# A hybrid decoder step on one core: stages placed by a clock of every engine's queue, and the sample recurrence in small tiles

## The chip, the cores and the metric

The kernel runs on one core of one Trainium2 chip. A core has TensorE (PE, matrix products into PSUM), VectorE (DVE), ScalarE (ACT), GpSimd (POOL) and SyncE (SP, which here issues the transfers). The metric is the device time of one execution in microseconds; the time given is the median of several runs. The profile shown is of one execution.

## The reference, cut to what matters

One layer is applied to a prompt of 1024 tokens and to a sample group of 8 sequences with 8 new tokens each, 1088 tokens in all. The order is: a SwiGLU feed-forward half step, a token mixer, a second SwiGLU half step, each followed by a layer norm.

```python
x = _layer_norm(ALPHA * x + 0.5 * _swiglu(x, ffn1_w13, ffn1_w2), ln1_g, ln1_b)
y, S, nk, nv = _mixer(x, S0, buf_k, buf_v, lb, w_in, attn_sink, attn_norm_g, hgrn_norm_g, w_out)
x = _layer_norm(ALPHA * x + y, ln2_g, ln2_b)
x = _layer_norm(ALPHA * x + 0.5 * _swiglu(x, ffn2_w13, ffn2_w2), ln3_g, ln3_b)
```

The mixer projects x to 22 groups of 128 columns. 8 attention heads with 2 key/value heads look at a window of 128 tokens. Four recurrent heads (HGRN2) keep a state S of 128 x 128 for each sequence:

```python
f = lb + (1.0 - lb) * sigmoid(hf);  logf = log(f);  k = 1.0 - f
# per chunk: b = cumsum(logf)
o = einsum('bthk,bhkv->bthv', qc * exp(b), S)
a = einsum('bthk,bshk,btshk->bhts', qc, kc, exp(b_t - b_s where s <= t))
o = o + einsum('bhts,bshv->bthv', a, vc)
S = exp(b_last)[..., None] * S + einsum('bshk,bshv->bhkv', kc * exp(b_last - b), vc)
```

Prompt states start at zero, sample states at the given S0. Both groups' outputs are normalised, gated, joined and multiplied by w_out.

## The kernel before, in words

**Layout and large products.** Tokens stand in three chunks of columns, 512, 288 and 288 (`CH`); the 64 sample tokens are columns 1024 to 1087. A large product splits both operands into a high and a low part and takes three products of these with `mmr` (line 207): high by high, high by low, low by high. `hilo` makes the two parts of a weight tile, a copy on ACT (L408) and a subtraction on DVE (L409). The feed-forward products use the Strassen-like seven-product scheme in most places (`seven`) and plain products elsewhere. Small products of the mixer are full float32 matmuls through `mm` (line 203), each of which the hardware shows as two matmul instructions, and transposes go through `tr` (line 211).

**The order of work.** All instructions are emitted by one Python program that keeps an estimated PE time `s.t`: every `mm`, `mmr` and `tr` adds its assumed length. The main stream is a list of units (`run`); in the mixer a unit is one 128-column projection, which `proj_group` computes chunk by chunk. Everything beside it is a `Side`, a Python generator: layer norms, attention blocks, the four recurrent heads, the splits of the mixer's results. A side runs until its next `yield x`, which says that its next stage is due `x` nanoseconds later on `s.t`. The main stream calls `poll` at each of its own yields, twice for each chunk of a projection (`mm3` yields after half the pieces, 12 matmuls); `poll` emits at most three due stages. PE works through its instructions in the order emitted, so a stage emitted before its operands are there makes PE wait, with the projections behind it. `need`, `until` and `room` emit stages at once when the main stream cannot go on.

**PSUM and rows.** Stages take PSUM banks from a pool of five (`st`), projections from one of three (`pt`). SBUF is used as 32 rows of 128 x 1152 floats; attention's tiles share the pool of weight tiles `hl`.

**Attention.** `attn_block` handles 128 prompt queries in stages: scores, exponentials, transposes and products with v, norm, transpose back. One block starts the next. `attn_sample` handles the sample tokens in four groups. The delays are numbers such as 400, 2100, 4500, 1200.

**The recurrent heads.** `hgrn(h)` starts when head h's F, Q and V projections are there. Within 128 tokens the decayed products are built by halving: first the diagonal (`hgrn_a`), then seven levels with blocks of 1, 2, 4 up to 64 tokens (`LEV`). At each level PE multiplies KL by QR for the blocks (`hgrn_b`; for the sample tokens at the first three levels `hgrn_c`, a product of 64 x 32 in its own bank). Then DVE multiplies half of QR by the decays (L1557), POOL half of KL (L1558), DVE forms the decays of the next level (L1564) and puts the level's products where they belong (L1573, L1583). The next level reads the new KL and QR. A level ends in `yield 1800.0`. Then KL is transposed, the chunk states are formed (`hgrn_d`) and the outputs (`hgrn_e`). For the sample tokens, eight products of a state with 8 columns of QR give a transposed result (`hgrn_f`), a copy to SBUF follows, and `hgrn_g` adds the part within the sequence and the transpose back. The new sample states are Ks times Ve, two products of 512 columns (`hgrn_i`); Ve holds the values of each sequence, masked by `em`, side by side.

**After the heads.** `wout_a` multiplies the attention half of the mix by w_out while head 3 is still running; `oa_split` and `oh_split` prepare these operands on ACT (L441) and DVE (L442). `wout_b` adds the recurrent half and starts the second layer norm.

## Time and profile before

| what | value |
|---|---|
| median of 3 runs | 2102.89 us (2102.34 to 2106.88) |
| the profiled execution | 2100.44 us, its span 2098.7 us |
| TensorE clock granted | 0.996 of full speed |
| PE busy | 2050.0 us, 98% of the span |
| DVE, ACT, POOL busy | 1214.9, 834.5, 178.3 us |

A busy row of PE counts overlapping matmuls once. A row such as `1024.00 2.94 PE pp L207 x12` of a timeline or of the chain gives the start, the length and the number of merged instructions; `[0.43 <-DVE Q L1557]` behind a row is idle time of its engine before it and what ended it. [...] A row of the waits gives the engine and line that waited, what released it, and total, times and longest in us.

### The profile page before, as it was taken

How to read it: one execution, taken by the hardware profiler on the slowest of the kernel's cores; microseconds unless marked ns; L12 is line 12 of the kernel's file. 1: busy time of each engine (PE TensorE's matmuls, PEld its weight loads, DVE VectorE, ACT ScalarE, POOL GpSimd, SP SyncE). 2: the span in 40 equal slices, each digit the busy share in tenths (PEclk: the TensorE clock that was granted, in tenths of full speed). 3: DMA queues.
4: the chain of work that ended last, by engine and by line, in shares of the span. 5: the costliest groups of instructions: out<-in, count | busy, mean ns of one | idle time of the engine just before them, and what ended most of it. 6: DMA issues, size and time to landing. Idle time of an engine off the chain costs nothing.

```text
span 2098.7 us, 40231 instructions
## 1 busy us (share of the span) xinstructions
PE 2050.0 (98%) x16089; PEld 1933.8 (92%) x16089; DVE 1214.9 (58%) x2463; ACT 834.5 (40%) x1886; POOL 178.3 (8%) x353
## 2 busy tenths in 40 slices
PE   8999999999999999999999999999999999999998
PEld 8999999998899999878888888998999999888997
DVE  7766555555357552465644767576666655444855
ACT  5443333334336443444443233454343333432521
POOL 0000000000020210022213201300000000000121
PEclk9999999999999999999999999999999999999999
DMA  6332222227357331101111132342222222655832
GB/s 236 96 103 88 88 75 80 70 81 236 118 165 237 90 111 62 31 22 39 36 53 38 47 124 64 105 139 83 88 83 95 91 78 74 209 159 165 272 104 93
DMA packets 126124, 221.97 MB, mean 106 GB/s; under 512 B 14336, under 2 KB 44032, under 8 KB 125920
## 3 DMA queue, kind: packets, MB, share of 16 engines
q1 hardware_dynamic: 125936, 219.39, 33.0%
q8 instruction: 126, 2.06, 0.4%
q14 instruction: 62, 0.51, 0.1%
HBM read 181.69 MB, written 38.63 MB: 105 GB/s over the span
## 4 chain that ended last, share of the span: by engine, by line
PE 40%; DVE 6%; ACT 2%; issue 2%; DMA 1%; POOL 1%; DVEq 0%; SPq 0%; ACTq 0%; POOLq 0%
PE py L207 13%; PE u L207 7%; PE y L207 5%; PE pp L207 5%; PE pg L207 2%; PE pu L207 2%; DVE hl L409 2%; PE z L207 1%; ACT hl L408 1%; PE nat L211 1%; PE hgrn_b L203 1%; PE hgrn_e L203 0%; PE attn_block_c L203 0%; DMA raw<-in_w2tb 0%; ACT ev L918 0%
## 5 line engine op out<-in xcount | busy, mean ns | idle before, releaser
L207 PE MATMUL py<-g,hl 128*128 128x288 f32 (+3 forms) x3234 | 540.9, 327 | 6.8 <-DVE hl L409 4.6
L207 PEld LDWEIGHTS py<-g,hl 128*128 128x128 f32 x3234 | 487.4, 188 | 55.0 <-DVE hl L409 9.5
L409 DVE TENSOR_TENSOR hl<-raw,hl 128x512 fp32r<-128x512 f32 (+1 forms) x600 | 387.8, 659 | 224.4 <-ACT hl L408 222.5
L408 ACT CAST hl<-raw 128x512 fp32r<-128x512 f32 (+1 forms) x600 | 351.7, 593 | 404.9 <-PE py L207 187.0
L207 PE MATMUL u<-T,hl 128*128 128x288 f32 (+1 forms) x2700 | 365.3, 291 | 6.0 <-ACT ev L1049 5.0
L207 PEld LDWEIGHTS u<-T,hl 128*128 128x128 f32 x2700 | 349.9, 189 | 10.0 <-ACT ev L1049 7.9
L207 PE MATMUL pp<-Xh,hl 128*128 128x288 f32 (+1 forms) x1056 | 272.2, 335 | 0.0
L207 PEld LDWEIGHTS pp<-Xh,hl 128*128 128x128 f32 x1056 | 182.7, 189 | 19.9 <-issue 5.0
L207 PE MATMUL pp<-Xl,hl 128*128 128x288 f32 (+1 forms) x528 | 173.1, 328 | 0.0
L634 POOL TENSOR_SCALAR lnt<-lnr,lnp 128x1 f32<-128x1 f32 (+1 forms) x81 | 41.2, 508 | 1510.8 <-DVE lnr L630 843.0
L918 ACT ACTIVATE ev<-ev 128x288 f32<-128x288 f32 (+1 forms) x150 | 65.0, 434 | 258.3 <-DVE ev L1054 171.4
L207 PE MATMUL z<-B,hl 128*128 128x288 f32 (+1 forms) x900 | 121.8, 290 | 2.1 <-DVE ev L1054 2.1
L207 PE MATMUL y<-T,hl 128*128 128x288 f32 (+1 forms) x900 | 122.0, 290 | 0.6 <-DVE T L467 0.6
L207 PE MATMUL u<-B,hl 128*128 128x288 f32 (+1 forms) x900 | 121.7, 290 | 0.0
L207 PE MATMUL y<-B,hl 128*128 128x288 f32 (+1 forms) x900 | 121.7, 290 | 0.0
L207 PEld LDWEIGHTS z<-B,hl 128*128 128x128 f32 x900 | 117.0, 189 | 2.3 <-DVE ev L1054 2.3
L207 PEld LDWEIGHTS y<-T,hl 128*128 128x128 f32 x900 | 117.1, 189 | 0.8 <-DVE T L467 0.8
L207 PEld LDWEIGHTS y<-B,hl 128*128 128x128 f32 x900 | 117.0, 189 | 0.0
L207 PEld LDWEIGHTS u<-B,hl 128*128 128x128 f32 x900 | 117.0, 189 | 0.0
L207 PEld LDWEIGHTS pp<-Xl,hl 128*128 128x128 f32 x528 | 99.8, 189 | 6.2
L409 DVE TENSOR_TENSOR hl<-S,hl 128x512 fp32r<-128x512 f32 x88 | 60.9, 692 | 74.8 <-ACT hl L408 74.4
L207 PE MATMUL py<-oH,hl 128*128 128x288 f32 (+1 forms) x384 | 96.5, 332 | 1.4 <-DVE Y L1836 1.4
(273 smaller groups left out, 2404.8 us busy)
## 6 DMA issues: line engine op xcount, KB each, us to landing
raw<-in_w13b SPq DMA_DIRECT2D x120, 256.0 KB, 3.2
raw<-in_w13a SPq DMA_DIRECT2D x108, 256.0 KB, 3.2
raw<-in_w2ta SPq DMA_DIRECT2D x75, 256.0 KB, 3.6
raw<-in_w2tb SPq DMA_DIRECT2D x75, 256.0 KB, 3.5
gd<-go SPq DMA_DIRECT2D x44, 288.0 KB, 3.2
raw<-gd SPq DMA_DIRECT2D x88, 144.0 KB, 3.3
gd<-go SPq DMA_DIRECT2D x44, 256.0 KB, 3.5
raw<-gd SPq DMA_DIRECT2D x44, 256.0 KB, 4.5
```

The source lines that it names most:

```text
L203: s.nc.tensor.matmul(out, lhsT, rhs, start=start, stop=stop, skip_group_check=cols > 1)
L207: s.nc.tensor.matmul(out, lhsT, rhs, start=start, stop=stop, skip_group_check=loose)
L211: s.nc.tensor.transpose(out, in_, ident)
L408: lambda: nc.scalar.copy(hl[:, 0, :nb], src),
L409: lambda: nc.vector.tensor_tensor(hl[:, 1, :nb], src, hl[:, 0, :nb].bitcast(F32), ALU.subtract),
L634: e.tensor_scalar(t, r, r, hp, ALU.mult, ALU.mult)
L918: nc.scalar.activation(si, ps, AF.Silu)
```

## The change

**Clock.** `Ker` gets a `Clock`, and its engines are wrapped (`Watch`) so that every instruction emitted is also booked. DVE, ACT, POOL and SP each have a time from which they are free. An operation is booked to start when its engine is free and 50 ns after the last booked write of its operands, and to take a length given by `COST`. Transfers are booked on SP and on one bus. `pe`, which `mm`, `mmr` and `tr` now call, moves `s.t` on to the booked arrival of the operands before it adds the matmul's length. `fresh` tells the clock when a pool's tile is reused.

**Stages.** Most yields in attention and in the recurrent heads no longer give a delay but the tiles that the next stage's matmuls read, and in many cases the number of PSUM banks that it takes. Such a stage is due 100 ns after these tiles are booked as written and when the banks are booked as free (`due`). Layer norms, the splits and the feed-forward parts keep their numbers.

**Assumed lengths.** Small matmuls on a quarter or half of the array (`cols`) are now counted at a quarter or half of their length in the scores of the sample attention and in the recurrence; before, these were counted in full. An `mmr` is counted 0.5 ns longer.

**Sample recurrence.** `hgrn_c` goes: the sample tokens are handled in two blocks of 32 tokens in the bank and the tile shape of `hgrn_b`, also in `hgrn_a`, and pass through a ninth column of D. `hgrn_f` and the copy behind it go: QR of the sample tokens is copied into `qm`, a zeroed tile in which each sequence's 8 columns have 32 of their own, and `hgrn_g` accumulates the state products directly, in two halves of 32 rows of its result. `hgrn_i` becomes two pairs of products of 32 rows of Ks with 256 columns of Ve, which is now half as wide.

The diff, cut to its core (the other yields of attention, `need`, `until`, `room` and `need_hl` change in the same way; other tile allocations get the `fresh` shown for attention's):

```diff
+class Clock:
...
+    def there(s, ap):
+        lo, hi = s.span(ap)
+        return max((t for a, b, t in s.wrote.get(ap.name, ()) if a < hi and b > lo), default=0.0)
...
+    def write(s, ap, t):
+        lo, hi = s.span(ap)
+        s.wrote[ap.name] = [x for x in s.wrote.get(ap.name, ()) if x[0] < lo or x[1] > hi] + [(lo, hi, t)]
+        s.use(ap, t)
...
+    def fresh(s, ap, tag, bufs):
+        q = s.tags.setdefault(tag, [])
+        q.append(ap.name)
+        if len(q) > bufs:
+            t = s.used.get(q.pop(0), 0.0)
+            s.wrote[ap.name] = [(0, 1 << 30, t)]
+            s.held[ap.name] = t
+        return ap
+    def soonest(s, tag, bufs, n=1):
+        q = s.tags.get(tag, [])
+        i = len(q) + n - 1 - bufs
+        return s.used.get(q[i], 0.0) if 0 <= i < len(q) else 0.0
...
+    def run(s, e, cost, outs, ins):
+        t = max([s.free[e]] + [s.there(x) + s.HOP for x in ins + outs]) + cost
+        s.free[e] = t
+        for x in ins:
+            s.use(x, t)
+        for x in outs:
+            s.write(x, t)
+        for x in ins + outs:
+            s.held[x.name] = t
...
+    def dma(s, out, in_):
+        t = max(s.free["SP"], s.there(in_) + s.HOP, s.there(out) + s.HOP) + 450.0
+        s.free["SP"] = t
+        n = 1
+        for a, b in out.ap:
+            n *= b
+        s.bus = max(s.bus, t + 800.0) + n * 4 / 330.0
+        s.use(in_, s.bus)
+        s.write(out, s.bus + 600.0)
...
+COST = dict(
+    DVE=lambda op, n: 160.0 + 0.62 * n if op in ("tensor_scalar", "tensor_copy", "memset") else 150.0 + 1.05 * n,
+    ACT=lambda op, n: 195.0 + 0.78 * n,
+    POOL=lambda op, n: 100.0 + 0.85 * n if op == "memset" else 340.0 if n == 1 else 190.0 + 2.7 * n,
+)
...
+        def g(*a, **k):
+            r = f(*a, **k)
+            if op == "dma_start":
+                s.clock.dma(a[0], a[1])
+                return r
+            aps = [x for x in [*a, *k.values()] if hasattr(x, "free_size")]
+            outs = [aps.pop(0)]
+            cost = COST[s.name](op, max(x.free_size() for x in [*outs, *aps]))
+            if "accum_out" in k:
+                outs.append(k["accum_out"])
+                cost += 190.0
+            s.clock.run(s.name, cost, outs, aps)
+            return r
...
+    def pe(s, out, lhsT, rhs, cost):
+        c = s.clock
+        t = max(s.t, c.there(lhsT) + c.HOP, c.there(rhs) + c.HOP, c.held.get(out.name, 0.0) + c.HOP)
+        s.wait(out, lhsT, rhs, t)
+        s.t = t + cost
+        c.use(lhsT, s.t)
+        c.use(rhs, s.t)
+        c.write(out, s.t + 200.0)
...
     def mm(s, out, lhsT, rhs, start, stop, cols=1):
         n = out.free_size()
-        s.t += 2 * (max(111.0, n * (2 / 2.4) + 24.0) if cols == 1 else (n * (2 / 2.4) + 24.0) / cols)
+        s.pe(out, lhsT, rhs, 2 * (max(111.0, n * (2 / 2.4) + 24.0) if cols == 1 else (n * (2 / 2.4) + 24.0) / cols))
         s.nc.tensor.matmul(out, lhsT, rhs, start=start, stop=stop, skip_group_check=cols > 1)
...
     def mmr(s, out, lhsT, rhs, start, stop, loose=False):
-        s.t += out.free_size() / 2.4 + 12.5
+        s.pe(out, lhsT, rhs, out.free_size() / 2.4 + 13.0)
...
         else:
-            d.ready = s.t + (lat or 0.0)
+            if lat is None or isinstance(lat, float):
+                d.ready = s.t + (lat or 0.0)
+            else:
+                d.banks = 0
+                d.ready = 0.0
+                for x in lat if isinstance(lat, tuple) else (lat,):
+                    if isinstance(x, int):
+                        d.banks = x
+                    else:
+                        d.ready = max(d.ready, s.clock.there(x) + 100.0)
+                return
+            d.banks = 0
...
+    def due(s, d):
+        return max(d.ready, s.clock.soonest("ps", 5, d.banks) if d.banks else 0.0)
...
         for d in list(s.sides):
-            if most and d.ready <= s.t:
+            if most and s.due(d) <= s.t:
...
             assert s.hl_live + s.as_live <= NHL, "scores"
-            pr = s.wh.tile([P, 2, 512], F32, tag="hl", name=s.nm("as"))
+            pr = s.clock.fresh(s.wh.tile([P, 2, 512], F32, tag="hl", name=s.nm("as")), "hl", NHL)
...
             if jp == 0:
-                yield 400.0
+                yield (2,)
...
-        yield 2100.0
+        yield nm
...
-        yield 4500.0
+        yield sx[0, 0][:, : 256 + w], 2
...
-            if q < 4:
-                yield 1200.0
+            if q < 3:
+                yield pb, sx[order[q + 1]][:, : 256 + w], 1
+            elif q == 3:
+                yield pb
...
-        yield 1000.0
...
+        yield KL, QR, 1
+        nc.gpsimd.memset(A, 0.0)
...
-                s.mm(ps[32 * b : 32 * b + 32, c * 32 : c * 32 + 32], KL[:, sl], QR[:, sl], True, True)
-        nc.vector.tensor_tensor(D, ps[:, :256].rearrange("p (c t) -> p c t", c=8), s.i32.unsqueeze(1).to_broadcast([P, 8, 32]), ALU.mult)
-        ps = s.st("hgrn_a_")
-        sl = slice(1024, 1088)
-        s.mm(ps[:64, :64], KL[:, sl], QR[:, sl], True, True)
-        nc.vector.tensor_tensor(A[:64, sl], ps[:64, :64], s.ident[:64, :64], ALU.mult)
+                s.mm(ps[32 * b : 32 * b + 32, c * 32 : c * 32 + 32], KL[:, sl], QR[:, sl], True, True, cols=4)
+        for b in range(2):
+            sl = slice(1024 + 32 * b, 1056 + 32 * b)
+            s.mm(ps[32 * b : 32 * b + 32, 256:288], KL[:, sl], QR[:, sl], True, True, cols=4)
+        nc.vector.tensor_tensor(D[:, :8], ps[:, :256].rearrange("p (c t) -> p c t", c=8), s.i32.unsqueeze(1).to_broadcast([P, 8, 32]), ALU.mult)
+        nc.vector.tensor_tensor(D[:64, 8], ps[:64, 256:288], s.i32[:64], ALU.mult)
         nc.vector.tensor_tensor(QR, QR, F, ALU.mult)
-        yield 4000.0
+        yield KL, QR, 1
...
-                        s.mm(ps[k0 : k0 + m, c * m : (c + 1) * m], KL[:, c0 : c0 + m], QR[:, c0 + m : c0 + 2 * m], True, True)
+                        s.mm(ps[k0 : k0 + m, c * m : (c + 1) * m], KL[:, c0 : c0 + m], QR[:, c0 + m : c0 + 2 * m], True, True, cols=64 // m)
...
-                    s.mm(ps[32 * b : 32 * b + 32, c * 16 : c * 16 + 16].rearrange("p (x m) -> p x m", m=m), KL[:, k0 : k0 + 32], v(QR[:, k0 : k0 + 32], 32, 1), True, True)
+                    s.mm(ps[32 * b : 32 * b + 32, c * 16 : c * 16 + 16].rearrange("p (x m) -> p x m", m=m), KL[:, k0 : k0 + 32], v(QR[:, k0 : k0 + 32], 32, 1), True, True, cols=4)
             if smp:
-                p2 = s.st("hgrn_c_")
-                s.mm(p2[:64, :32].rearrange("p (x m) -> p x m", m=m), KL[:, 1024:1088], v(QR[:, 1024:1088], 64, 1), True, True)
+                for b in range(2):
+                    k0 = 1024 + 32 * b
+                    s.mm(ps[32 * b : 32 * b + 32, 128:144].rearrange("p (x m) -> p x m", m=m), KL[:, k0 : k0 + 32], v(QR[:, k0 : k0 + 32], 32, 1), True, True, cols=4)
...
-                yield 1800.0
+                yield KL, QR, 1
...
+            for q, r in ((P, slice(0, 8)), (64, slice(8, 9)))[: 2 if smp else 1]:
+                k = r.stop - r.start
+                nc.vector.copy_predicated(
+                    D[:q, r].rearrange("p c (x u m) -> p c x u m", u=2, m=m)[:, :, :, 1],
+                    s.l32[:q, li].rearrange("p (x m) -> p x m", m=m).unsqueeze(1).to_broadcast([q, k, 16 // m, m]),
+                    ps[:q, r.start * 16 : r.stop * 16].rearrange("p (c x m) -> p c x m", c=k, m=m),
+                )
...
+                    nc.scalar.copy(A[bs, :1024].rearrange("p (c t) -> p c t", c=8)[:, :, bs], D[bs, :8])
+                    if b < 2:
+                        nc.scalar.copy(A[bs, 1024 + 32 * b : 1056 + 32 * b], D[bs, 8])
...
-            yield 1800.0
+            yield KL, QR, 1
...
-        yield 1300.0
+        yield F, Vn, 1
...
-            yield 1500.0
+            if g == 0:
+                yield 400.0
+            else:
+                yield A, S[:, :384], 1
...
-            yield 200.0
-        ps = s.st("hgrn_f_")
-        for b in range(8):
-            s.mm(ps[:, b * 8 : (b + 1) * 8], S0[:, b * P : (b + 1) * P], QR[:, 1024 + 8 * b : 1032 + 8 * b], True, True)
-        it = s.t2("it")
-        nc.scalar.copy(it[:, :64], ps[:, :64])
-        yield 500.0
+            if g == 0:
+                yield S, 1
+        nc.vector.tensor_copy(s.qm.rearrange("p g (b x) -> p g b x", b=4)[:, :, :, :8], QR[:, 1024:1088].rearrange("p (g b t) -> p g b t", g=2, b=4))
+        yield s.qm, S0, 1
         ps = s.st("hgrn_g_")
-        s.mm(ps[:64, :P], A[:64, 1024:1088], Vs, True, False)
-        s.mm(ps[:64, :P], it[:, :64], s.ident, False, True)
+        for b in range(5):
+            for g in range(2):
+                out = ps[32 * g : 32 * g + 32, :P]
+                if b == 0:
+                    s.mm(out, A[:64, 1024 + 32 * g : 1056 + 32 * g], Vs, True, False, cols=2)
+                else:
+                    x = (4 * g + b - 1) * P
+                    s.mm(out, s.qm[:, g, 32 * b - 32 : 32 * b], S0[:, x : x + P], False, b == 4, cols=2)
         ons = s.mx.tile([64, P], F32, tag="ons", name=s.nm("ons"))
         nc.scalar.mul(ons, ps[:64, :P], 0.5)
         nc.scalar.activation(ps[:64, :P], ons, AF.Square, accum_out=ss[:64, 8:9])
         s.flush(last)
         Ve = S
...
-        nc.gpsimd.tensor_tensor(Ve[:64, :1024].rearrange("p (b v) -> p b v", b=8), Vs.unsqueeze(1).to_broadcast([64, 8, P]), s.em.unsqueeze(2).to_broadcast([64, 8, P]), ALU.mult)
+        nc.gpsimd.tensor_tensor(Ve[:64, :512].rearrange("p (b v) -> p b v", b=4), Vs.unsqueeze(1).to_broadcast([64, 4, P]), s.em.unsqueeze(2).to_broadcast([64, 4, P]), ALU.mult)
...
-        yield 1500.0
+        yield ss
...
-        yield 2800.0
+        yield r5
...
-        yield 2500.0
+        yield on, ons, 3
...
-        yield 2000.0
+        yield Ve, 2
+        pss = [s.st("hgrn_i_") for q in range(2)]
+        for x in (slice(0, 256), slice(256, 512)):
+            for q in range(2):
+                r = slice(32 * q, 32 * q + 32)
+                s.mm(pss[q][:, x], Ks[r], Ve[r, x], True, True, cols=2)
         for q in range(2):
-            ps = s.st("hgrn_i_")
-            s.mm(ps, Ks, Ve[:64, q * 512 : (q + 1) * 512], True, True)
+            ps = pss[q]
...
```

More of the change, by code (lines that the diff above doesn't have):

```diff
@@ L92, with __init__, span, use @@
 NRAW = 7
+class Clock:
+    HOP = 50.0
+    def __init__(s):
+        s.free = dict(DVE=0.0, ACT=0.0, POOL=0.0, SP=0.0)
+        s.bus = 0.0
+        s.wrote = {}
+        s.used = {}
+        s.held = {}
+        s.tags = {}
+    @staticmethod
+    def span(ap):
+        p = ap.ap
+        st = abs(p[0][0])
+        if str(ap.space).endswith("DRAM"):
+            return ap.offset, ap.offset + sum(abs(a) * (b - 1) for a, b in p) + 1
+        o = ap.offset % st if st else ap.offset
+        return o, o + sum(abs(a) * (b - 1) for a, b in p[1:]) + 1
+    def there(s, ap):
[5 more added lines that the diff above has]
+        s.use(ap, t)
+    def use(s, ap, t):
+        s.used[ap.name] = max(s.used.get(ap.name, 0.0), t)
+    def fresh(s, ap, tag, bufs):
[28 more added lines that the diff above has]
+        s.write(out, s.bus + 600.0)
@@ new lines, with __init__, __getattr__ @@
+COST = dict(
[3 more added lines that the diff above has]
+)
+class Watch:
+    def __init__(s, clock, name, engine):
+        s.clock = clock
+        s.name = name
+        s.engine = engine
+    def __getattr__(s, op):
+        f = getattr(s.engine, op)
+        def g(*a, **k):
[11 more added lines that the diff above has]
+            return r
+        return g
@@ L95, with __init__ @@
+class Engines:
+    def __init__(s, clock, nc):
+        s.vector = Watch(clock, "DVE", nc.vector)
+        s.scalar = Watch(clock, "ACT", nc.scalar)
+        s.gpsimd = Watch(clock, "POOL", nc.gpsimd)
+        s.sync = Watch(clock, "SP", nc.sync)
+        s.tensor = nc.tensor
 class Side:
@@ L138, in __init__ @@
         s.tc = tc
-        s.nc = tc.nc
+        s.clock = Clock()
+        s.nc = Engines(s.clock, tc.nc)
         s.uid = 0
@@ L252, in until @@
         while not true():
-            r = [x for x in s.sides if x.ready <= s.t]
+            r = [x for x in s.sides if s.due(x) <= s.t]
             if not r:
-                s.t = min(x.ready for x in s.sides)
+                s.t = min(s.due(x) for x in s.sides)
                 continue
@@ L292, in room @@
                 raise AssertionError(("rows", s.live, n))
-            r = [x for x in s.sides if x.ready <= s.t] or [min(s.sides, key=lambda x: x.ready)]
-            s.t = max(s.t, r[0].ready)
+            r = [x for x in s.sides if s.due(x) <= s.t] or [min(s.sides, key=s.due)]
+            s.t = max(s.t, s.due(r[0]))
             s.stage(r[0])
@@ L392, in need_hl @@
         assert s.sides, "weight tiles"
-        r = [x for x in s.sides if x.ready <= s.t] or [min(s.sides, key=lambda x: x.ready)]
-        s.t = max(s.t, r[0].ready)
+        r = [x for x in s.sides if s.due(x) <= s.t] or [min(s.sides, key=s.due)]
+        s.t = max(s.t, s.due(r[0]))
         s.stage(r[0])
@@ L400, in raw @@
     def raw(s):
[L401 removed]
+        return s.clock.fresh(s.wr.tile([P, 4, P], F32, tag="raw", name=s.nm("raw")), "raw", NRAW)
     def hilo(s, src, nb=4, now=True):
         nc = s.nc
[L406 removed]
+        hl = s.clock.fresh(s.wh.tile([P, 2, 4, P], F32R, tag="hl", name=s.nm("hl")), "hl", NHL)
         steps = [
```

62 lines of the change are left out of this document (28 added, 34 removed).

## The prediction

> **What bounds the kernel now.** I read the page first, then the idle time by stretch, then PE's own waits, then PE's order of work inside the mixer.
>
> ```profile
> span 2098.7 us, 40231 instructions
> PE 2050.0 (98%) x16089; PEld 1933.8 (92%) x16089; DVE 1214.9 (58%) x2463; ACT 834.5 (40%) x1886; POOL 178.3 (8%) x353
> ```
>
> PE is busy 98% of the span, so only two things can shorten it: less matmul time, or less of the 49 us in which PE stands. Here is where it stands (columns: stretch, its length, busy time of PE, weight load, DVE, ACT, POOL):
>
> ```profile
> 840.00:1240.00 400.00, 387.45 (x4195) 337.77 (x4194) 234.13 (x566) 165.46 (x503) 89.02 (x148) 1.00 0.14 46
> 1300.00:1450.00 150.00, 140.25 (x1119) 137.49 (x1117) 107.02 (x206) 69.76 (x134) 16.78 (x42) 0.99 0.36 115
> ```
>
> The first stretch is the mixer, which the change edits: 12.6 us idle in 400. The second, the start of the second FFN, has 9.75 us and no edit. PE's waits from 780 to 1300 us (total, times, longest):
>
> ```profile
> PE hgrn_b L203 <- POOL KL L1558: 3.1, 3, 1.9
> PE attn_block_e L211 <- DVE sden L1422: 1.8, 1, 1.8
> PE attn_sample_c L211 <- DVE ss L1425: 1.7, 1, 1.7
> PE hgrn_b L203 <- DVE Q L1557: 1.7, 2, 1.2
> PE py L207 <- DVE Y L1836: 1.4, 2, 1.0
> PE attn_sample_d L203 <- ACT ssq L1463: 1.1, 1, 1.1
> PE nat_a L211 <- ACT V L1264: 1.1, 1, 1.1
> PE py L207 <- DVE oL L442: 0.4, 1, 0.4
> ```
>
> Placing of stages decides 3.1 + 1.7 (recurrence) + 1.8 + 1.7 + 1.1 (attention) = 9.4 us. The rest follows a projection or the output product, which the change does not move. So better placing can bring 9.4 us at most.
>
> **The change, term by term: PE work.** Each head's tail for the sample sequences, at head 3:
>
> ```profile
> 1210.51 1.85 PE L203 MATMUL hgrn_f<-Q,S 128*128 128x8 f32 x16
> 1212.21 0.48 PE L207 MATMUL py<-oH,hl 128*128 128x512 f32 x1
> ...
> 1213.75 0.43 PE L203 MATMUL hgrn_g<-Vs,A 64*64 64x128 f32 x2
> ...
> 1214.47 0.40 PE L207 MATMUL py<-oH,hl 128*128 128x288 f32 x1
> ...
> 1227.05 1.98 PE L203 MATMUL hgrn_i<-KL,Ks 64*128 64x512 f32 x4
> 1228.96 0.50 PE L207 MATMUL py<-oH,hl 128*128 128x512 f32 x1
> ```
>
> From start to the next start, hgrn_f holds PE for 1.70 us, hgrn_g for 0.72 and hgrn_i for 1.91. A level of the recurrence:
>
> ```profile
> 1169.90 0.74 PE L203 MATMUL hgrn_b<-Q,KL 128*32 128x16 f32 x64
> 1170.57 0.30 PE L203 MATMUL hgrn_c<-Q,KL 128*64 128x32 f32 x2
> 1170.80 0.40 PE L207 MATMUL pp<-Xh,hl 128*128 128x288 f32 x1
> ```
>
> 64 matmuls in four column groups take 0.67 us (10.5 ns each); the two of hgrn_c, in another tile, take 0.23. Neighbours for the new tiles:
>
> ```profile
> 887.72 0.44 PE L203 MATMUL attn_sample_b<-cache,qs 64*32 64x128 f32 x8
> 887.97 0.31 PE L203 MATMUL attn_sample_b<-kT,qs 64*32 64x64 f32 x8
> ...
> 961.22 0.39 PE L203 MATMUL hgrn_e<-KL,Q 128*128 128x128 f32 x2
> 961.44 0.39 PE L203 MATMUL hgrn_e<-Vn,A 128*128 128x128 f32 x2
> ...
> 1023.19 0.38 PE L203 MATMUL attn_block_a<-kT,qT 64*128 64x256 f32 x1
> 1023.19 0.38 PE L203 MATMUL attn_block_b<-kT,qT 64*128 64x256 f32 x1
> 1023.40 0.38 PE L203 MATMUL attn_block_a<-kT,qT 64*128 64x256 f32 x1
> ```
>
> A 128-column f32 matmul alone takes 0.11 us (0.22 for two); eight in four column groups take 0.25, 0.031 each. Two 256-column matmuls on different rows of the array start together, the next pair 0.21 later.
>
> - hgrn_f goes and hgrn_g becomes ten products, 20 matmuls of 128 columns in two column groups. One after another that is 2.2 us; twice the four-group price, 0.062 each, gives 1.2. I take 1.2, the nearer kind of row. Saved per head: 1.70 + 0.72 - 1.2 = 1.2, for four heads 4.9 us; bounds 0.9 (no overlap) and 5.7 (full overlap, 1.1, and one visit between projection matmuls less, 0.1).
> - hgrn_i becomes 8 matmuls of 256 columns in two groups of 32 rows with a PSUM bank each: four pairs, 0.85 us, if 32-row groups pair as the 64-row ones do. Saved 1.06 a head, 4.2 us; bounds 0.8 (8 x 0.21) and 4.4. New weights for each matmul are no reason for a loss: the paired rows load them too and keep 0.21.
> - hgrn_c goes at three levels in each head; four matmuls at 10.5 ns take its place: 0.23 - 0.04 = 0.19, times 12, 2.3 us; bounds 2.2 and 2.8. The sample's two matmuls in hgrn_a are worth under 0.1 a head and are left out.
>
> Sum: 4.9 + 4.2 + 2.3 = **11.4 us**, bounds 3.9 and 12.9. The changed price of small matmuls in attention's scores and the fourth tile argument elsewhere move only the clock, not PE.
>
> Off PE, each head loses a copy on ACT (it) and half of POOL's Ve, and gains a small copy on DVE (qm) and two on ACT into A. I cost these at nothing: between 840 and 1240 us DVE is busy 234 of 400 us and ACT 165. With no cover they would delay the next matmuls of that head by their own length, and projections stand behind these in PE's queue. No DMA is added; S0's load and the stores of Sp and Ss go to SP with their stage, and SP carries little here (46 GB/s).
>
> The two small matmuls of hgrn_c, in another tile shape than those before them, took 0.23 us where two of hgrn_b take 0.02. [...]
>
> **The change: placing.** The old delays are fixed numbers on a clock that counts a 16-column matmul at 222 ns for its two halves where PE needs 21, so it ran some 6.5 us ahead at each level. It did not matter, since a level's own matmuls are counted before its delay of 1800 ns starts. The new clock books each operation on its engine, and a stage goes out at the first poll after its operands are there; polls come every 12 projection matmuls, four of six in a unit after 288 columns and two after 512:
>
> ```profile
> 1024.00 2.94 PE pp L207 x12
> 1033.27 3.38 PE pp L207 x24
> ```
>
> so 1.7 us (3.38 for 24) or 2.9. What a level really needs (PE start, then the multiplies that the next level reads):
>
> ```profile
> 1100.24 0.74 PE L203 MATMUL hgrn_b<-Q,KL 128*32 128x16 f32 x64
> 1101.30 1.84 POOL L1558 TENSOR_TENSOR KL<-KL,F 128x544 f32<-128x544 f32 x1 [1.20 <-PE hgrn_c L203]
> 1101.60 2.13 DVE L1557 TENSOR_TENSOR Q<-Q,F 128x544 f32<-128x544 f32 x1
> 1103.87 0.73 PE L203 MATMUL hgrn_b<-Q,KL 128*32 128x16 f32 x64 [0.43 <-DVE Q L1557]
> 1104.97 1.97 POOL L1558 TENSOR_TENSOR KL<-KL,T 128x544 f32<-128x544 f32 x1 [1.82 <-PE hgrn_c L203]
> ...
> 1111.99 0.74 PE L203 MATMUL hgrn_b<-Q,KL 128*32 128x16 f32 x64
> 1112.88 2.04 POOL L1558 TENSOR_TENSOR KL<-KL,F 128x512 f32<-128x512 f32 x1 [2.04 <-PE hgrn_b L203]
> ```
>
> From PE's start to the last operand: 3.5 us (1101.60 + 2.13 - 1100.24), 3.1 (1106.94 - 1103.87) and 2.9 (1114.92 - 1111.99); without hgrn_c some 0.2 less in the first two: 3.3, 2.9, 2.9. The old rule asked for 1.8 us after the matmuls, so two short polls or one long, at least 3.6 us from start to start. The new clock is too hopeful in two ways. Its multiply waits for the last write of its operands, not for PE to have read them, so it may book KL's multiply before the matmuls that read the old KL. And it lets DVE and POOL run side by side at 0.72 and 1.66 us (its formulas at 544 columns), where the rows show 2.13 and 1.84 when they overlap. Working its rules through a plain run of levels, the next is due 0.9 to 2.2 us after a level's start, while the first short poll comes at 2.2 by its prices: mostly caught there, unless a weight split or evacuation stands before it on DVE. Really that is 0.67 + 1.7 + about 0.1 for re-entry = 2.45 us, 0.4 to 0.8 too soon, say 0.6.
>
> Four heads have 28 such steps, two thirds (19) before short polls; with three in five caught at the first, 11 x 0.6 = 6.7 us of stall in place of 4.8. In attention the clock follows the queues and asks for a free PSUM bank: I take 2.5 for 4.6, near the middle since its prices for small ACT and DVE operations are low. Total 9.2 for 9.4: **nothing gained by placing**, with bounds of 9.4 gained (all stalls gone) and 17 lost (28 steps x 0.8 + 4.6 - 9.4 = 17.6).
>
> Profiled execution 2100.44 us (span 2098.7 and 1.74 around it) - 11.4 - 0.2 = 2088.8. The runs shown are 2102.34, 2102.89 and 2106.88, a little above the profiled one; I place the median at **2090 us**.
>
> **Rivals.**
> - Placing works: the clock's queues are close enough that 2 us of the 9.4 remain: 2090 - 7 = **2083**. For it: steps in the trace without a wait are the majority. Against: DVE and POOL above.
> - Tiles do not overlap: 3.9 instead of 11.4, 2090 + 7.5 = **2097.5**. Against it stand the paired rows at 1023.19; for it, that no 32-row or two-group 128-column tile ran before.
> - The clock, which now stops for modelled waits everywhere, also shifts feeder stages at the start of the second FFN, where DVE is busy 107 of 150 us; if the 9.75 us idle there doubles: **2100**. For it, the delays there count on that clock; against, their code is untouched.
> - Slower: every level goes out at its first poll, and DVE and POOL delay each other there. 28 x 0.8 = 22.4 us of stall plus attention's 4.6, 17.6 more than now, against 11.4 saved: 2102.9 + 6.2 = **2109**. It decides from (11.4 + 9.4 - 4.6) / 28 = 0.6 us a step, which is what I expect for a third of them. This row speaks for it, with DVE subtractions (L442) running at that time:
>
> ```profile
> 1181.38 2.75 DVE L442 TENSOR_TENSOR oL<-qT,oH 128x512 fp32r<-128x512 f32 x6
> ...
> 1181.90 3.93 POOL L1558 TENSOR_TENSOR KL<-KL,F 128x512 f32<-128x512 f32 x1 [2.34 <-PE hgrn_b L203]
> ```
>
> Against it: long polls (one third) leave 3.6 us, and work booked on DVE pushes some levels on by a poll. [...]
>
> **Chances.** Forecast 0.52, placing works 0.17, no overlap 0.10, second FFN 0.08, slower 0.13. What tells from no change is about 0.2%, 4.2 us. Faster: 0.50 + 0.17 + 0.06 + 0.03 = 0.76; within 0.02 + 0.04 + 0.05 + 0.04 = 0.15; slower 0.09. The forecast's own range is 2084 to 2096; 2079 to 2101 takes in the better placing and the lost overlap and leaves out the slow case, some 0.16 above and 0.03 below.
>
> **What would show it.** No hgrn_f or hgrn_c; hgrn_g about 1.2 us and hgrn_i about 0.9 a visit (2.2 and 1.7 refute the overlap). PE's waits on KL and Q together near 7 us with pieces of 0.4 to 0.8; under 3 refutes my view of the clock, over 20 is the slow case. Attention's waits near 2.5. Idle of 1300 to 1450, shifted by the gain, still near 10. I am wrong if the span falls by less than 6 or more than 18 us.

## The result, and the profile after

The changed kernel takes **2084.55 us** (median of 4 runs, 2081.06 to 2086.30), the kernel before 2104.31 in the runs beside it: a ratio of 0.9905, with an interval of 0.9893 to 0.9918. The forecast was 2090 with a range of 2079 to 2101, so the time lies inside, but 5.5 us below the forecast and closest to the rival in which placing works (2083).

The profiled execution took 2085.64 us, against 2100.44 before. That pair differs by 14.8 us and the medians by 19.8, because the profiled run of before lay 3.9 us under its median and this one 1.1 over. The page of the changed kernel:

```profile
span 2083.7 us, 40360 instructions
...
PE 2039.4 (98%) x16137; PEld 1928.1 (93%) x16137; DVE 1213.5 (58%) x2467; ACT 834.1 (40%) x1890; POOL 176.0 (8%) x354
```

The span fell by 15.0 us. PE's busy time fell by 10.6, its idle time from 48.7 to 44.3. A single profile gives this split only to some 3 us: in a second profile of this kernel (the whole change again, below) the span is 2083.3, PE is busy for 2036.4 and idle for 46.9. By stretch (length, then PE, weight load, DVE, ACT, POOL, granted clock, DMA), the mixer and the start of the second FFN, which now begins 18.2 us earlier (its first matmul that waits for B starts at 1284.47 us, before at 1302.67):

```profile
840.00:1220.00 380.00, 374.70 (x4254) 330.50 (x4252) 231.15 (x571) 164.04 (x507) 86.49 (x148) 1.00 0.15 48
1280.00:1430.00 150.00, 141.80 (x1112) 139.31 (x1112) 107.50 (x207) 69.87 (x133) 16.91 (x42) 0.97 0.35 118
```

The mixer's idle time went from 12.6 to 5.3 us; the second stretch still has 8.2 (9.75 before, 9.7 in the second profile of this kernel). PE's waits from 780 to 1300 us (in this kernel the wrapped engines record every DVE, ACT and POOL instruction at one line, L187, so the tile's name has to do):

```profile
...
PE hgrn_b L334 <- POOL KL L187: 1.2, 1, 1.2
PE hgrn_b L334 <- issue: 1.0, 1, 1.0
...
PE attn_block_b L334 <- ACT sp L187: 0.9, 1, 0.9
PE hgrn_b L334 <- DVE Q L187: 0.9, 2, 0.5
PE py L338 <- DVE oL L187: 0.4, 1, 0.4
PE attn_block_d L342 <- DVE as L187: 0.3, 1, 0.3
```

The recurrence waits 2.1 us (KL and Q) instead of 4.8, attention 1.2 instead of 4.6. The 1.0 us of "issue" has no releaser in the trace; it may be missing records, and the second profile of this kernel does not have it. PE's order around the new tiles, by start and length:

```profile
1151.06 0.80 PE L334 MATMUL hgrn_a<-Q,KL 128*32 128x32 f32 x68
1151.78 0.50 PE L338 MATMUL pp<-Xh,hl 128*128 128x512 f32 x1
...
1154.73 0.77 PE L334 MATMUL hgrn_b<-Q,KL 128*32 128x16 f32 x68
1155.43 0.40 PE L338 MATMUL pp<-Xh,hl 128*128 128x288 f32 x1
...
1193.17 0.41 PE L334 MATMUL hgrn_g<-Vs,A 64*32 64x128 f32 x4
1193.51 1.07 PE L334 MATMUL hgrn_g<-S,qm 128*32 128x128 f32 x16
1194.51 0.50 PE L338 MATMUL py<-oH,hl 128*128 128x512 f32 x1
...
1211.35 1.13 PE L334 MATMUL hgrn_i<-KL,Ks 32*128 32x256 f32 x8
1212.41 0.40 PE L338 MATMUL py<-oH,hl 128*128 128x288 f32 x1
```

A matmul's row is longer than the time to the next start (at 1195.54 us one of 512 columns has 0.39, and the next starts at 1195.77), so the time for which work holds PE is read from its start to the start of what follows, which is called a visit below. hgrn_g holds PE for 1.34 us, hgrn_i for 1.06, a level with sample tokens for 0.70 (0.90 before) and hgrn_a for 0.72 (0.95 before, from its first start to the next projection's).

### The profile page after: what moved, and what is told of

It is laid out like the page before. It is cut to its first block, busy times and chain, and to the rows that moved or that the text cites. A ratio compares the mean times of both kernels' runs of the same rounds, so it can differ in the third digit from the quotient of the medians.

```text
span 2083.7 us, 40360 instructions
## 1 busy us (share of the span) xinstructions
PE 2039.4 (98%) x16137; PEld 1928.1 (93%) x16137; DVE 1213.5 (58%) x2467; ACT 834.1 (40%) x1890; POOL 176.0 (8%) x354
## 4 chain that ended last, share of the span: by engine, by line
PE 41%; DVE 6%; ACT 2%; issue 2%; DMA 1%; POOL 0%; DVEq 0%; ACTq 0%; POOLq 0%; SPq 0%
PE py L338 14%; PE u L338 7%; PE y L338 5%; PE pp L338 5%; PE pg L338 2%; PE pu L338 2%; PE z L338 2%; DVE hl L187 2%; ACT hl L187 1%; DVE ev L187 1%; PE nat L342 1%; ACT ev L187 1%; DVE Y L187 1%; DVE S L187 1%; PE hgrn_b L334 1%
## 5 line engine op out<-in xcount | busy, mean ns | idle before, releaser
L187 DVE TENSOR_TENSOR hl<-raw,hl 128x512 fp32r<-128x512 f32 (+1 forms) x600 | 392.9, 667 | 230.8 <-ACT hl L187 228.8
L187 ACT CAST hl<-raw 128x512 fp32r<-128x512 f32 (+1 forms) x600 | 351.5, 592 | 413.2 <-PE py L338 193.8
L187 POOL TENSOR_SCALAR lnt<-lnr,lnp 128x1 f32<-128x1 f32 (+1 forms) x81 | 42.4, 524 | 1514.5 <-DVE lnr L187 841.8
L187 ACT ACTIVATE ev<-ev 128x288 f32<-128x288 f32 (+1 forms) x150 | 65.0, 434 | 258.0 <-DVE ev L187 258.0
L187 ACT COPY ev<-u 128x288 f32<-128x288 f32 (+1 forms) x225 | 86.2, 383 | 58.8 <-PE u L338 57.7
L187 DVE TENSOR_TENSOR ev<-y,ev 128x288 f32<-128x288 f32 (+1 forms) x150 | 66.1, 441 | 70.8 <-PE y L338 40.4
L187 DVE SCALAR_TENSOR_TENSOR Y<-Y,py 128x288 f32<-128x288 f32 (+3 forms) x49 | 25.2, 522 | 137.8 <-PE py L338 137.8
```

What stands on the lines that cost most here:

```text
L187: r = f(*a, **k)
```

## The experiments

### Tiles and clock apart

Four kernels on one chip: the new tiles with the old delays and the old counting; the same with small matmuls counted at what they take; the clock with the old tiles; and the whole change again. Tiles alone, against the change (all yields of the stages go back so):

```diff
-        yield KL, QR, 1
+        yield 1800.0
...
-        yield o, 1
+        yield 700.0
```

Counted truly, against tiles alone:

```diff
-        s.t += 2 * max(111.0, n * (2 / 2.4) + 24.0) if cols != 5 else 2 * (n * (2 / 2.4) + 24.0) / 4
+        s.t += 2 * (max(111.0, n * (2 / 2.4) + 24.0) if cols == 1 else (n * (2 / 2.4) + 24.0) / cols)
```

Clock alone, against the change (all of the sample recurrence goes back):

```diff
-        yield s.qm, S0, 1
+                yield QR, S0, 1
+        ps = s.st("hgrn_f_")
+        for b in range(8):
+            s.mm(ps[:, b * 8 : (b + 1) * 8], S0[:, b * P : (b + 1) * P], QR[:, 1024 + 8 * b : 1032 + 8 * b], True, True)
...
```

> The sample recurrence in small tiles, with the old delays and the old counting of PE time; no clock. If the two halves of the change add, as the prediction's sum has it, PE's busy time falls by about 11 us and the time by 11 (ratio 0.995), while PE's waits on stages beside the projections stay near 9 us. If the tiles only pay together with the new placing (the rival), the stages that lost hgrn_f come earlier and wait: gain under 6 us (ratio above 0.997).

> As the one before, and small matmuls are counted at their true length, as the change does; still the old delays and no queues. If the gain in waits comes from the queue model, this stays near the tiles alone: 11 us (0.995), waits near 9 us. If it came from counting PE's time rightly, this reaches nearly the whole change: 16 us or more (0.9925 or less), waits near 4 us.

> The clock and the new yields with the old tiles (hgrn_c, hgrn_f and the wide hgrn_i are back). If the halves add, placing alone gains 5 to 9 us (ratio 0.9957 to 0.9976), PE busy stays near 2050 and the waits fall to about 4. By the prediction as it was written, placing brings nothing: ratio 0.999 to 1.001.

> The changed kernel once more beside the others: ratio 0.9905, within 0.989 to 0.992. The sum of the two halves as measured beside it should come within 3 us of it if they add.

| kernel | median, us | against before (2103.6) | ratio, interval |
|---|---|---|---|
| new tiles, old delays | 2100.86 | -2.7 | 0.9990 (0.9982 to 0.9999) |
| the same, small matmuls counted at what they take | 2103.33 | -0.3 | 1.0000 (0.9992 to 1.0009) |
| clock, old tiles | 2094.87 | -8.7 | 0.9958 (0.9946 to 0.9970) |
| the whole change | 2084.08 | -19.5 | 0.9910 (0.9897 to 0.9923) |

By the prediction's sum the tiles alone bring some 11 us and the clock alone nothing; both are refuted. The parts do not add: 2.7 + 8.7 is 11.4, together they give 19.5. On top of the clock the tiles bring 10.8 us, nearly all that their matmuls save (11.0, worked out in the section on the prediction). On top of the old delays they bring 2.7. The page and PE's waits of the kernel with tiles alone show where the rest went:

```profile
PE 2040.7 (97%) x16137; PEld 1927.4 (92%) x16137; DVE 1216.7 (58%) x2467; ACT 834.3 (40%) x1890; POOL 172.5 (8%) x354
```

```profile
PE attn_block_e L211 <- DVE ao L1372: 7.7, 3, 2.9
PE hgrn_b L203 <- DVE Q L1561: 2.5, 3, 1.5
...
PE attn_block_e L211 <- DVE sden L1425: 1.9, 1, 1.9
PE attn_sample_c L211 <- DVE ss L1428: 1.8, 1, 1.8
PE attn_sample_d L203 <- ACT ssq L1466: 1.3, 1, 1.3
```

The span is 2098.9 us. PE is 9.3 us less busy than before, near the 10.6 of the whole change, and its idle time has risen by 9.5 (2098.9 - 2040.7 = 58.2 against 48.7). Attention, which the tiles do not touch, now waits 12.7 us where it waited 4.6: its last transposes come while the scaled output `ao` still stands in DVE's queue. My reading is that the fixed delays fitted the old order and a shorter recurrence put these stages at other polls; longer delays, below, test it. This mixer also has 10.2 us at half clock where before has 3.4 (last section). Counting small matmuls truly, without the rest of the clock, does not mend it. With the clock and the old tiles these waits are gone:

```profile
PE hgrn_b L334 <- POOL KL L187: 1.9, 1, 1.9
...
PE hgrn_b L334 <- DVE F L187: 0.7, 1, 0.7
PE attn_block_b L334 <- ACT sp L187: 0.6, 1, 0.6
PE hgrn_b L334 <- DVE Q L187: 0.3, 1, 0.3
```

Of the 9.4 us of such stalls 3.5 are left, 2.9 in the recurrence and 0.6 in attention. The time fell by 8.7, more than the 5.9 of stalls that went. With nat_a's wait of 1.1, which is gone too, they make 7.0; in this trace the second FFN's first matmul that waits for B starts 7.9 us earlier (1294.79). The rest is not explained: the half clock of the last section does not do it, as this mixer has one such stretch, like before.

### Where the clock is needed

The changed kernel with the old fixed delays in the recurrent heads only, and with the old ones in attention only (the clock still books and counts everything in both). In the recurrent heads:

```diff
-            yield KL, QR, 1
+            yield 1800.0
...
-        yield F, Vn, 1
+        yield 1300.0
```

In attention:

```diff
-        yield o, 1
+        yield 700.0
...
-            yield x, 1
+            yield 900.0
```

> The changed kernel with the old fixed delays back in the recurrent heads; attention keeps the clock. The tiles alone lost their gain mostly to waits of attention's last transposes. If attention is what the clock has to place, this keeps most of the change: ratio 0.992 to 0.994, waits of attention under 2 us, waits of the recurrence 3 to 6. If the fault of the fixed delays is general, it falls to 0.996 or more.

> The reverse: attention with its old fixed delays, the recurrent heads by the clock. If attention's placing carries the gain: ratio 0.996 to 1.000 with 6 us or more of waits in attention. If the recurrence's placing carries it: 0.993 or less.

With the clock in attention alone the time is **2085.20** (before: 2103.18, ratio 0.9914, 0.9901 to 0.9927), not to be told from the whole change. With the clock in the recurrence alone it is 2097.42 (0.9970, 0.9958 to 0.9982). PE's waits in the latter:

```profile
PE attn_block_e L342 <- DVE ao L187: 5.1, 3, 2.4
...
PE attn_sample_c L342 <- DVE ss L187: 2.3, 2, 1.3
```

and in the former:

```profile
PE hgrn_b L334 <- POOL KL L187: 3.2, 3, 1.6
...
PE hgrn_h L342 <- DVE A L187: 2.2, 1, 2.2
...
PE hgrn_b L334 <- DVE Q L187: 1.4, 2, 1.1
```

The gain of placing is made in attention. On top of that, the clock in the recurrence changes the waits on KL and Q from 4.6 to 2.1 us and the time by nothing that these runs can tell. Without the clock in attention it may be worth something: 2097.42 is 3.4 us under the tiles alone (2100.86), but that pair also differs in how PE's time is counted.

### The slow rival, made on purpose

Every level of the recurrence is due as soon as the one before it is out, so that it leaves at the next poll (at both places where a level ends).

```diff
-                yield KL, QR, 1
+                yield 0.0
```

> The changed kernel with each level of the recurrence due at once after the level before (fixed delay 0). This is the slow rival of the prediction: 14 of 28 steps then follow within 2 us, where the clock leaves 4. At 0.6 us for each early step and up to 3 for those emitted without any projection between, waits of the recurrence rise from 3 to 10 to 20 us and the ratio to 0.995 to 1.000. If a level's operands are ready sooner than I read from the trace, it stays within 0.2% of the change (0.9925 or less).

The time is 2103.55 (ratio 1.0000, 0.9990 to 1.0009), 19 us above the change. PE's waits:

```profile
PE hgrn_b L334 <- DVE F L187: 11.2, 4, 4.5
PE hgrn_b L334 <- POOL KL L187: 4.9, 3, 3.8
PE hgrn_b L334 <- DVE Q L187: 2.4, 3, 1.3
```

The levels now stand 18.5 us instead of 2.1. The slow rival had counted 28 steps of 0.8 us, 22.4; here ten waits make 18.5, so its total is near, but by luck, with too many steps and each too cheap. Its 4.6 for attention is 0.5 here (one wait of attn_block_d for F), and its 2109 us lies above the 2103.55. Part of the 19 us is lost at half clock: this mixer has 20.5 us of it (last section). In the change the rival's condition never came. The change's clock seldom sends a level out early. From each level's start to the next one's, and from the last level's to the transposes behind it, there are 28 steps in four heads; in the trace of the change 24 of them take 2.9 us or more, mostly 3.4 to 5.4, and four less (2.50 to 2.87). The kernel's own clock `s.t`, as it emits the stages, says the same for the third head (us from the end of one level's matmuls to the start of the next one's, the last entry to the transposes; then the same in the kernel made early):

```
change   3.4  2.5  1.6  1.6  5.4  3.6  1.6
early    2.9  2.5  1.6  1.6  0.0  2.7  3.2
```

In all, 4 of the 28 steps are booked within 2 us in the change and 14 in the early kernel. I had taken 11.

### A clock that is truer, and one that is more careful

One kernel books what I had called too hopeful: a multiply also waits until PE has read the operand that it overwrites, DVE operations with two SBUF inputs and POOL operations are booked one after the other, and POOL's price is lowered to what it takes undisturbed (190 + 1.68 ns an element). In the trace of before, POOL's multiply of 512 columns takes 1.05 us at 1037.87, with DVE idle, and 2.04 at 1112.88, with DVE at work; that the two never run side by side is an assumption, which no run shows. The other leaves the clock alone and asks for 700 ns after the operands instead of 100. The truer clock, in the booking of an operation:

```diff
-        t = max([s.free[e]] + [s.there(x) + s.HOP for x in ins + outs]) + cost
+        t = max([s.free[e]] + [s.there(x) + s.HOP for x in ins + outs] + [s.read.get(x.name, 0.0) + 150.0 for x in outs])
+        sb = [x for x in ins if not str(x.space).endswith("PSUM") and x.free_size() > 1]
+        lock = sb if e == "POOL" else len(sb) > 1 if e == "DVE" else None
+        if lock:
+            t = max(t, s.port)
...
```

The margin:

```diff
-                        d.ready = max(d.ready, s.clock.there(x) + 100.0)
+                        d.ready = max(d.ready, s.clock.there(x) + 700.0)
```

> The changed kernel with a clock that also waits for PE to have read what is overwritten, keeps DVE operations with two SBUF inputs and POOL operations apart, and counts POOL at its undisturbed length (190 + 1.68 ns an element). No step follows within 2 us (4 do in the changed kernel). If booking these two things was the flaw that matters, the recurrence's waits of 3 us go and the ratio falls to 0.9885 to 0.990. If the levels then only come later and the change was already loose enough, it is the same within 0.1% or slower by the end of head 3.

> The changed kernel with one number changed: a stage whose operands the clock books is due 700 ns after they are booked as written, not 100. Theory of the prediction (the clock is some 0.6 us too hopeful at a step): the waits left in the mixer, 2.1 us in the recurrence and 1.2 in attention, go, and the time falls by 2 to 3 us to about 2082. Rival (the clock's hope does not cost now, and the margin only brings each step a poll later): waits fall a little, but the chains of head 3 and the output product end later, and the time is 2084 to 2090.

The truer clock takes **2091.18** (0.9946, 0.9932 to 0.9960) and is slower than the change. The margin takes **2087.15** (0.9918, 0.9906 to 0.9931); its interval and that of the change overlap, so it is only shown not to gain. PE's waits with the truer clock, and then with the margin:

```profile
PE py L348 <- DVE oL L196: 3.6, 4, 2.1
PE attn_block_e L352 <- DVE ao L196: 3.6, 1, 3.6
```

```profile
PE py L338 <- DVE oL L187: 2.8, 3, 1.6
```

The waits on KL and Q go to nothing and to 0.3, as wanted, but the levels come later (steps booked up to 8.9 us apart in the truer clock), head 3 ends later (its hgrn_i starts at 1228.7 and 1216.8 us, in the change at 1211.4), and the output product waits for `oL`: 0.4 us in the change, 3.6 and 2.8 here. I read this so: an early step costs its own stall, a late one is paid at the end of the chain. It is not the whole loss of the truer clock: there attention's last transposes wait 3.6 us for `ao`, where the trace of the change shows no such wait, and a stretch at half clock goes with each of the longest waits for `ao` (3.6 us) and `oL` (2.1) (last section).

### Could longer numbers have done it?

The kernel with tiles alone, with four delays of attention lengthened by hand:

```diff
-            yield 2200.0
+            yield 3000.0
...
-            yield 900.0
+            yield 2400.0
...
-        yield 700.0
+        yield 3000.0
...
-        yield 600.0
+        yield 1800.0
```

> The new tiles with the old fixed delays (2100.9 us, PE waits of 7.7 us for ao, 1.9 for sden, 1.8 for ss and 1.3 for ssq in attention), with four delays of attention made longer by hand: 700 to 3000 ns ahead of the block's last transposes, 2200 to 3000 and 900 to 2400 in the sample groups, 600 to 1800 ahead of attn_sample_d. Theory (what the tiles save comes back as stalls of these stages, because they come too early): these waits fall from 12.7 to under 4 us, and the time falls by 7 to 10 us, to about 2092, near what clock and tiles give. Rival (fixed numbers only move the stall: the stages behind come at other polls and find DVE or ACT busy there): the waits named fall, others rise by as much, the time stays within 2098 to 2103.

The time falls to 2095.25 (0.9955, 0.9943 to 0.9968), 5.6 us under tiles alone: between the two expectations. PE's waits:

```profile
PE attn_block_d L211 <- ACT qT L1378: 2.0, 2, 1.2
PE hgrn_b L203 <- DVE F L1568: 1.9, 2, 1.2
...
PE attn_sample_a L203 <- ACT sp L1434: 1.3, 1, 1.3
```

The four waits of 12.7 us are gone, which confirms that these stages came too early; 5.2 us of others stand in new places (qT, F and sp, where tiles alone had none). The theory holds for the cause and the rival for half of its size: a number mends the stall it is set for and shifts the next, which the clock's due times follow.

### What makes the tiles overlap

First the same products in another order, one group of columns (hgrn_g) or rows (hgrn_i) after the other; then, in one kernel, hgrn_g in runs of two products in heads 1 and 2, and hgrn_i with all products on the same 32 rows in heads 0 and 3. In these two heads the new states of sequences 4 to 7 are then formed from rows of sequences 0 to 3, so this kernel serves for its visits and not for its time (one run, 2086.91 us). The turned order:

```diff
-        for b in range(5):
-            for g in range(2):
+        for g in range(2):
+            for b in range(5):
...
-        for x in (slice(0, 256), slice(256, 512)):
-            for q in range(2):
+        for q in range(2):
+            for x in (slice(0, 256), slice(256, 512)):
```

By head:

```diff
-        for b in range(5):
-            for g in range(2):
+        for b, g in [(b, g) for bb in (((0,), (1,), (2,), (3,), (4,)) if h in (0, 3) else ((0, 1), (2, 3), (4,))) for g in range(2) for b in bb]:
...
-                r = slice(32 * q, 32 * q + 32)
+                r = slice(0, 32) if h in (0, 3) else slice(32 * q, 32 * q + 32)
```

> The changed kernel with the order of its small products turned: all ten matmul instructions of one half of hgrn_g's rows, then all of the other half; in hgrn_i both products of one group of 32 rows, then both of the other. The work is the same. Theory (overlap comes from neighbours on different parts of the array): hgrn_g goes from 1.34 us a visit to about 2.2 (20 x 0.11), hgrn_i from 1.06 to about 1.8 (8 x 0.21), so 1.6 us a head, PE busy up by some 6 us, and the time from 2084.5 to about 2090.5. Rival (the tile shape alone sets the price of a matmul, whatever runs beside it): visits stay at 1.34 and 1.06 and the time within 2 us of the changed kernel's.

> The changed kernel with two things altered by head, to be read from visits, not from the time. In heads 0 and 3 all eight matmul instructions of hgrn_i work on the same 32 rows (the new states of sequences 4 to 7 are then formed from rows of sequences 0 to 3, so this part is not what the reference computes); heads 1 and 2 keep two groups of 32 rows. In heads 1 and 2 hgrn_g does two products of one half of its rows, then two of the other; heads 0 and 3 alternate after each product. On hgrn_i: if TensorE pairs different rows, also when they do not alternate, the visits of heads 0 and 3 take about 1.9 us (8 x 0.21 and the entry) against 1.06 in heads 1 and 2; if a product on 32 rows is cheap by its shape alone, all four take 1.06. On hgrn_g: if it looks ahead over four instructions (two products), heads 1 and 2 stay at 1.34 us; if only over direct neighbours, they come near 2.2 to 2.6, or in between if it overlaps only where the halves change.

The turned order takes 2087.97 (0.9926, 0.9912 to 0.9939), about 3.5 us more than the change, where I expected 6. The intervals of the two overlap a little, so the visits have to tell. Its timeline at head 3:

```profile
1195.25 0.40 PE L334 MATMUL hgrn_g<-Vs,A 64*32 64x128 f32 x2
...
1197.90 0.50 PE L338 MATMUL py<-oH,hl 128*128 128x512 f32 x1
...
1214.72 1.14 PE L334 MATMUL hgrn_i<-KL,Ks 32*128 32x256 f32 x8
1215.79 0.40 PE L338 MATMUL py<-oH,hl 128*128 128x288 f32 x1
```

hgrn_g loses its overlap (2.65 us for 1.34), hgrn_i keeps all of it (1.07 for 1.06): theory and rival are each right for one of the two. By head:

```profile
979.94 1.99 PE L334 MATMUL hgrn_i<-KL,Ks 32*128 32x256 f32 x8
981.86 1.10 PE L334 MATMUL attn_block_c<-vn,pT 128*128 128x64 f32 x8
...
1130.26 0.40 PE L334 MATMUL hgrn_g<-Vs,A 64*32 64x128 f32 x2
...
1131.26 1.06 PE L334 MATMUL hgrn_g<-S,qm 128*32 128x128 f32 x14
1132.25 0.40 PE L338 MATMUL pp<-Xh,hl 128*128 128x288 f32 x1
```

On the same 32 rows (head 0) hgrn_i takes 1.92 us, so its 1.06 is the overlap of two row groups and not the price of a small tile; and since the turned order keeps it, TensorE overlapped them also with four instructions of one group ahead of the other's. The last 14 instructions of hgrn_g take 0.99 us, as much as 0.22 + 0.44 + 0.22 and a change of tile (0.11): the runs of four overlap here too. What costs hgrn_g in both orders are more changes between its 64-row and its 128-row tile, three instead of one, and that these two timelines show no overlap across such a change: the first six instructions by head take 1.00 us, about six of 0.11 and three changes, and the 2.65 of the turned order are about twenty of 0.11 and four changes, the last one to the projection's tile.

## Why the prediction was right or wrong

- **PE work, 11.4 us: right, 11.0 by the visits, in part by luck.** The three terms of the sum come to 10.1, and a fourth that it left out brings 0.9. hgrn_g and hgrn_f: 2.42 - 1.34 = 1.08 a head, 4.3 (4.9 predicted). The overlap in two column groups is there in full (16 instructions of 0.055 us), and the change from the 64-row to the 128-row tile costs about 0.12 twice a visit, for which the forecast's sum has no term: 0.34 for four of 0.055, 1.00 for sixteen. hgrn_i: 1.91 - 1.06 = 0.85, 3.4 (4.2): the pairs come at 0.21 as taken, and the visit has some 0.2 of entry that I left out. (The lower bound given for this term, 0.8, is 0.9 by its own rows: four times 1.91 - 8 x 0.21.) hgrn_c: 0.20 x 12 = 2.4 (2.3). hgrn_a: 0.23 a head, 0.9, where I had put under 0.1 a head; it is the same second tile as hgrn_c, and I should have priced it by that row. The row of hgrn_c, 0.23 us in another tile where two of hgrn_b take 0.02, put a change of tile at some 0.2; in hgrn_g it costs 0.11 to 0.12.
- **Off PE at nothing: held.** No wait on qm, ons or A stands in the list of the change.
- **"Nothing gained by placing": this step failed.** Stalls of the mixer went from 9.4 to 3.3 us (2.1 and 1.2), not to 9.2, and nat_a's 1.1 went with them. The waits on KL and Q are under the 3 us that the prediction named as refuting its view of the clock. The result lies at the very edge of the forecast's own 2084 to 2096; the wider range holds it with room because it was drawn to take in better placing. Two terms were wrong. "Three in five caught at the first" short poll, 11 steps, was worked out for a plain run of levels; in the kernel four steps are early, and the waits are 2.1 where 6.7 was expected. The evacuations and weight splits booked on DVE before the multiplies are the likely reason that most due times fall past that poll; which of them do it was not taken apart. And 2.5 for attention, chosen as a middle, was 1.2. The flaws named in the clock were not what decided: with both mended (b_honest) the kernel is 6 to 7 us slower.
- **The terms were not independent.** The forecast subtracts the tiles' saving whatever the delays. With the old delays it would have been nearly lost (2.7 of 11). Placing is worth 8.7 us with the old tiles and 16.8 with the new (2100.86 - 2084.08). This size appears in no step of the prediction, which called 9.4 us the most that better placing can bring.
- **The sum of the profiled pair.** 11.0 of PE work, 6.1 of stalls and nat_a's 1.1 make 18.2, and the second FFN starts 18.2 us earlier; that the two agree to the tenth is chance, since smaller waits moved too and before has a stretch at half clock in its mixer that the change has not (last section). The span fell by only 15.0. Some 1 us of the 3.2 is lost at the start of the second FFN, where the granted clock was 0.97 in this trace against 0.99 before. The other 2.2 us are lost at the end of that FFN, at full clock: the same 509 matmuls take 80.0 us before (from 1912.0) and 82.2 in the change (from 1894.9), with 4.2 and 5.9 us of waits for weights (`hl`) and `g`. In the second profile of the change the clock at the start is 0.99, and the span still falls by only 15.4. The prediction had no term for either.
- **Rivals.** Placing works, 2083, is what happened, 1.5 us from the median; it had 0.17. No overlap is refuted by 1.34 and 1.06. The second FFN's start has 8.2 us idle, not twice 9.75. The slow case had its condition wrong; made so (b_eager), the kernel takes 2103.55 us, not 2109, and its stalls come near the forecast only by luck.

## What to carry to other kernels

When PE is 98% busy and its order is fixed by hand-set delays, a saving of PE time is not yet a saving of the kernel: look which stages land at other polls, because the saved time can return as idle at a stage that the edit never touched. Delays worked out from booked queues keep such a saving, and where only one part is placed so, look first at the one whose chains are long and varied (attention in this kernel), before the one with a regular beat. A model that is somewhat hopeful can beat a truer or a more careful one, since a late step is paid at the end of its chain: measure early and late on purpose before believing either.

## What the runs showed of the hardware

**Half clock for 3.41 us behind a short stall.** First three pieces of the mixer of before, 3.41 us each (PE's busy time is the second number, the granted clock the third from the end), then PE's timeline behind a wait in the kernel with tiles alone:

```profile
919.51:922.92 3.41, 1.73 (x15) 1.26 (x14) 2.10 (x7) 1.03 (x4) 1.03 (x1) 1.00 0.00 0
922.92:926.34 3.42, 3.42 (x11) 2.40 (x8) 2.79 (x6) 0.23 (x1) 0.00 (x0) 0.50 0.00 0
...
1015.08:1018.49 3.41, 2.12 (x78) 2.05 (x78) 2.63 (x3) 0.53 (x3) 2.25 (x2) 1.00 0.02 5
```

```profile
873.57 0.40 PE L207 MATMUL pp<-Xl,hl 128*128 128x512 f32 x1
...
874.26 0.39 PE L207 MATMUL pp<-Xl,hl 128*128 128x512 f32 x1
...
876.78 0.71 PE L211 MATMUL attn_block_e<-ident,ao 128*128 128x128 f32 x4 [1.91 <-DVE sden L1425]
...
879.14 0.63 PE L207 MATMUL pp<-Xl,hl 128*128 128x512 f32 x1
...
880.42 0.49 PE L207 MATMUL pp<-Xl,hl 128*128 128x512 f32 x1
```

Three matmuls of 512 columns take 0.69 us before the wait of 1.91 and 1.28 after it. Busy time hides this: PE is busy for all of the piece at 0.50. By my estimate, half of 3.41, such a stretch costs up to 1.7 us beside the stall itself. The mixers of the 14 traces have 16 of them, of 3.41, 6.83 or 10.24 us; each begins within 2 us of the end of a wait of 1.1 us or more (the shortest single one was 1.45), though not each such wait goes with one.

In each trace all of them begin on one raster, whole multiples of 3.41 us apart (in before at 922.92 us, and the next one, behind the mixer, at 1312.04, 114 such pieces on), and what goes with half clock in these traces is PE's idle time within one piece of this raster. Of the mixers' 2059 pieces at full clock, all 14 with 1.6 us idle or more are followed by half clock, 2 of the 9 with 1.45 to 1.6, and none of the 2036 with less. So in before the wait of 1.69 us for ss, which lies in one piece (from 919.51), is followed by half clock, and the longer one of 1.87 for KL, which the raster cuts at 1015.08 into 0.58 and 1.29, is not. Outside the mixer some pieces with up to 1.9 us idle were followed by full clock (in before the one from 1428.09, with 1.81), so these counts give no sharp bound.

The change has no stretch at half clock in the mixer, before has one, the early kernel three. The prediction priced a stall at its length; by the estimate above, the wait of 1.91 us cost up to 3.6 with the half clock behind it. I didn't run a kernel in which only the length or the place of one stall is changed, so all this is read from traces.

**Two row groups overlapped without alternating.** Two groups of 32 rows overlapped with four instructions of one ahead of the other's, 1.07 us against 1.92 on one group (c_serial and d_groups). What went with a loss of overlap was a change of tile form inside the product: hgrn_g took 2.65 us (c_serial) and 1.99 (d_groups) with three such changes and 1.34 with one (the change).
